# The end of norm 2 and the first gate products in another written order

## The chip, the cores and the metric

One core of a Trainium2 chip runs the kernel. The metric is the device time of one execution in microseconds (us). Before the change the median of three timed executions is 1270.69 us (1270.49 to 1272.03).

## The reference

One decoder layer on 1024 rows of 1024 numbers in float32. What matters here is its second half:

```
x = x + einsum('bse,ed->bsd', mixed, w_out)        # output projection, residual
h = rms_norm(x, ffn_norm_g)                        # norm 2
g = einsum('bsd,df->bsf', h, w_gate)
u = einsum('bsd,df->bsf', h, w_up)
x = x + einsum('bsf,fd->bsd', silu(g) * u, w_down)
return rms_norm(x, final_norm_g)
```

with 2816 hidden columns. Ahead of it stand norm 1, the input projection and two kinds of attention.

## The kernel before

*Split operands.* Every float32 operand of a product is split in two: a high part (a cast on ScalarE, name ending in h) and a low part (the operand less its high part, ending in l). A product is then three matmuls per 128 rows of the contraction: high by high, high by low, low by high. `operand` (L705) does it for a weight block (oh, ol), `hi_part` and `lo_part` (L744, L747) for a row block's slice of a large operand.

*Gate and up products.* They go by pairs of 128 hidden columns, 11 pairs, gate (m = 0) and up (m = 1). Each is a Strassen scheme of seven products instead of eight. h, transposed, is seen as 2 by 2 halves: r12 and r22 hold h12 and h22, and the seven right-hand operands are 11, 21, 22, T1 = h12 - h11, T2 = h22 - T1, T3 = h22 - h12 and T4 = h21 - T2; each has a high and a low tile. `product` (L865) runs twelve matmuls (contraction 512, 512 rows) into one PSUM bank. The left-hand operands are four weight blocks a11, a21, a12, a22 and sums s1, s2 of them, made on GpSimd. `strassen` (L951) does a pair; the first pair is done by `strassen_first` (L970), for which the products on 22 and T3 of both m run ahead ("held"), as they need only the upper four row blocks.

*Norm 2.* The loop from L830 goes over the row blocks (128 rows) in the order 7, 6, 5, 4, 0, 1, 2, 3. Step n does the second half of the output projection for its block (two banks of twelve matmuls), adds the residual on VectorE, squares and sums on ScalarE (L135), raises to the power -1/2 on GpSimd (L137), and, one step later, scales (`normed`, L822, two halves; the gain lies in two PSUM banks, g_at). Two steps later TensorE transposes the block (`transposed`, L753, four 128 by 128 transposes to a bank) and `second_half` (blocks 4 to 7) or `first_half` (0 to 3) makes the operands; part of that runs later, on GpSimd (`late`). `first_half_below` (L787) makes 21 and T4. `early_sum` (L799) makes weight sums for the held products, in between.

*PSUM.* Eight banks: three in ps_s, two in ps_p, two in ps_t and one in ps_v. g_at holds the one of ps_v and one of ps_t until the last `normed`. After norm 2 the last three become ps_d.

*What sets the order.* Inside `tc.manual_schedule` (L829 to L901) the instructions of TensorE, VectorE, ScalarE and GpSimd run on each engine in the order in which the program writes them; each engine takes its queue strictly in that order. Outside it a planner at compile time orders them by its own estimates. DMA issues on SP's queue are left to the planner throughout: a load waits for its buffer (two buffers, tag wr, for weights).

Of the kernel before, what the change touches and what calls it, by code (L numbers as in the profile page):

```python
# [11 lines left out]
F32 = mybir.dt.float32  # L12
F32R = mybir.dt.float32r
AF = mybir.ActivationFunctionType
ALU = mybir.AluOpType
# [57 lines left out]
def layer(ctx: ExitStack, tc: tile.TileContext, x, mix_g, w_in, b_forget, lq1, lk1, lq2, lk2,  # L73
# [687 lines left out]
    def second_half(t, pvs):  # L761

        A.copy(at(r12, t), pvs[0])
        hi_part("22", t, pvs[1])
        A.copy(at(r22, t), pvs[1])
        t3 = temp(t % 2 * 2)
        V.tensor_sub(t3, pvs[1], at(r12, t))
        lo_part("22", t, pvs[1], V)
        hi_part("T3", t, t3)
        return lambda: lo_part("T3", t, t3, G)  # L770

    def first_half(t, pvs):


        hi_part("11", t, pvs[0])
        t1 = temp(t % 2 * 2)
        V.tensor_sub(t1, at(r12, t), pvs[0])
        lo_part("11", t, pvs[0], V)
        hi_part("T1", t, t1)

        def pool():
            G.tensor_sub(at(r22, t), at(r22, t), t1)
# [12 lines left out]


    w_first, w_sums, early = {}, {}, [[], []]
# [19 lines left out]
    for nh in range(2):  # L817
        A.copy(g_at[nh], gb2[:, nh * 512:nh * 512 + 512])
    temps.append(bp.tile([P, 2, 512], F32, tag="b", name="temps"))
    rs = {}  # L820

    def normed(tb):  # L822
        for nh in range(2):
            cs = slice(nh * 512, nh * 512 + 512)
            V.scalar_tensor_tensor(xns[tb][:, cs], x2[tb // 2][:, tb % 2, cs], rs[tb], g_at[nh],
                                   ALU.mult, ALU.mult)

    manual = tc.manual_schedule(engines=NORM_MAN)
    manual.__enter__()  # L829
    for n, tb in enumerate(order):  # L830
        xt = x2[tb // 2][:, tb % 2]
        for nh in range(2):
            cs = slice(nh * 512, nh * 512 + 512)
            ps = ps_s.tile([P, 512], F32, tag="s", name="pso")
            out_matmuls((4, 5, 6, 7), w2[nh], tb, ps)
            if nh == 0 and n >= 2:
                t = order[n - 2]
                pvs = [transposed(t, q) for q in range(2 if t >= 4 else 1)]
            V.tensor_add(xt[:, cs], ps, xa_half(tb, nh))
            if nh == 0:  # L840
                if n >= 1:
                    normed(order[n - 1])
                if n >= 2:
                    late = (second_half if t >= 4 else first_half)(t, pvs)
                if plan.get(n - 1, (0, 0))[1]:
                    early[plan[n - 1][0]].append(operand(temp(1)))
# [4 lines left out]
        if n >= 2:  # L851
            late()
        if n in plan:
            early_sum(*plan[n])
        if n == 1:
# [27 lines left out]
    pvs = [transposed(2, 0)]  # L883
    normed(3)
    first_half(2, pvs)()
    held[0][1] = product(early[0][1], "T3", SS)
    pvs = [transposed(3, 0)]
    first_half(3, pvs)()
    a_first = [operand(w_first[0][0])]
    for t in range(4):  # L890
        lo_part("T2", t, at(r22, t), G)
    held[1][0] = product(early[1][0], "22", SS)
    pvs = [transposed(t, 1) for t in (0, 1)]
    for t in (0, 1):
        first_half_below(t, pvs[t])
    held[1][1] = product(early[1][1], "T3", PJ)
    pvs = [transposed(t, 1, (TT, PJ)) for t in (2, 3)]
    a_first.append(operand(w_first[0][2]))
    for t in (2, 3):
        first_half_below(t, pvs[t - 2])  # L900
# [68 lines left out]

    def strassen_first(takes):  # L970

        for m, take in enumerate(takes):
            a11, a21, a12, a22 = w_blocks(m, 0) if m else w_first[0]
            s1, s2 = w_sums[m]
            p1, u2, u3 = kept_tiles()
            A.copy(p1, product(a_first[0] if m == 0 else operand(a11), "11"))
            take(0, 0, product(a_first[1] if m == 0 else operand(a12), "21"), p1)
            ps5 = product(operand(s1), "T1")
            ps = product(operand(s2), "T2")
# [5 lines left out]
            take(1, 0, product(operand(a22), "T4"), u3)  # L985

    for pair in range(NF // 2):
        me = V if pair == NF // 2 - 1 else G
# [253 lines left out]
```

## Time and profile before

| | us |
|---|---|
| median of 3 timed runs | 1270.69 |
| the profiled execution | 1268.52 |
| its span, first to last instruction | 1266.8 |
| TensorE busy | 1222.2 (96%) |
| VectorE busy | 857.3 (68%) |
| GpSimd busy | 710.5 (56%) |
| ScalarE busy | 576.1 (45%) |

The changed stage lies between 554 and about 664 us of the span: the loop over row blocks to 604, the held products and what is left of the operands to 629, the first pair to 663. A matmul's busy time overlaps the next one's, so a start-to-start distance is the better measure. An entry of a timeline ends with the idle time of the engine ahead of it and the instruction that ended the wait.

### The profile page before, as it was taken

What the parts mean: (1) busy time and instruction counts of PE and PEld (TensorE: products, weight loads), DVE (VectorE), ACT (ScalarE), POOL (GpSimd) and SP (SyncE); (2) the same over time, 40 slices, a digit from 0 to 9 for tenths busy, and PEclk for the clock granted to TensorE, in tenths of its full rate; (3) what the DMA queues carried; (4) which work ended last, traced back from release to release, by engine and by line L of the source; (5) the groups of instructions that cost most, each with busy time, mean ns of one, the idle gap of its engine ahead of it and who ended that gap; (6) DMA issues with size and microseconds to landing.
All of it is one profiled execution on the core that took longest, in us unless ns stands there. A gap on an engine that the chain in (4) does not pass through costs nothing.

```text
span 1266.8 us, 18426 instructions
## 1 busy us (share of the span) xinstructions
PE 1222.2 (96%) x6341; PEld 1039.2 (82%) x6341; DVE 857.3 (68%) x1617; ACT 576.1 (45%) x1227; POOL 710.5 (56%) x653
## 2 busy tenths in 40 slices
PE   8999999999999998989699999999999998999997
PEld 7889988987898877878578888888888886788886
DVE  5556766757786789757656565566565668878765
ACT  5345546646675666545433332233332345434424
POOL 2322333233104363235558777777777758999973
PEclk9999999999999999999999999999999999999999
DMA  6231223031202234032123443323233357735313
GB/s 217 64 109 43 72 69 84 26 98 45 51 8 80 59 137 175 14 117 96 37 89 111 133 144 123 100 83 109 100 108 124 101 183 236 219 119 179 98 57 133
DMA packets 93373, 131.42 MB, mean 104 GB/s; under 512 B 7584, under 2 KB 56288, under 8 KB 93280
## 3 DMA queue, kind: packets, MB, share of 16 engines
q1 hardware_dynamic: 91984, 126.32, 31.2%
q10 hardware_dynamic: 1296, 3.94, 0.8%
q8 instruction: 50, 0.82, 0.3%
q14 instruction: 43, 0.35, 0.1%
HBM read 93.75 MB, written 30.18 MB: 98 GB/s over the span
## 4 chain that ended last, share of the span: by engine, by line
PE 81%; POOL 6%; DVE 5%; issue 3%; DMA 3%; ACT 2%; SPq 0%; POOLq 0%; ACTq 0%; DVEq 0%
PE pst L873 31%; PE psd L1095 14%; PE psv L230 6%; PE pso L602 4%; PE pv L375 4%; PE tp L390 3%; PE s L330 2%; PE s L331 2%; POOL unit L1066 2%; POOL tw L1050 1%; PE psq_f1q L293 1%; PE psq_d2q L293 1%; PE psq_f2q L293 1%; PE psq_d3k L293 1%; PE psq_f1k L293 1%
## 5 line engine op out<-in xcount | busy, mean ns | idle before, releaser
L1095 PE MATMUL psd<-unit 128*128 128x512 f32 x924 | 211.5, 390 | 4.9 <-DVE x L1107 3.9
L1095 PEld LDWEIGHTS psd<-unit 128*128 128x128 f32 x924 | 172.8, 188 | 43.4 <-DVE x L1107 5.2
L1066 DVE TENSOR_TENSOR unit<-araw,unit 128x512 fp32r<-128x512 f32 x77 | 104.3, 1383 | 32.4 <-ACT unit L1065 19.8
L710 DVE TENSOR_TENSOR ol<-st,oh 128x512 fp32r<-128x512 f32 x84 | 91.2, 1087 | 42.8 <-ACT oh L709 41.6
L334 ACT ACTIVATE pt<-pt,mn 128x896 f32<-128x896 f32 (+7 forms) x128 | 99.4, 777 | 44.1 <-DVE mn L332 42.0
L709 ACT CAST oh<-st 128x512 fp32r<-128x512 f32 x84 | 50.9, 619 | 148.9 <-POOL st L724 108.6
L397 DVE TENSOR_TENSOR pl<-tp,ph 128x512 fp32r<-128x512 f32 (+1 forms) x120 | 75.2, 633 | 44.9 <-ACT ph L396 44.2
L396 ACT CAST ph<-tp 128x512 fp32r<-128x512 f32 (+1 forms) x120 | 64.1, 541 | 62.6 <-PE tp L390 53.7
L997 POOL TENSOR_TENSOR sg<-sg,cc 128x512 f32<-128x512 f32 x44 | 65.8, 1496 | 43.6 <-ACT sg L996 37.9
L710 DVE TENSOR_TENSOR ol<-raw,oh 128x512 fp32r<-128x512 f32 x66 | 64.9, 984 | 35.1 <-ACT oh L709 35.0
L1065 ACT CAST unit<-araw 128x512 fp32r<-128x512 f32 x77 | 47.4, 619 | 75.2 <-PE psd L1095 40.6
L422 POOL TENSOR_SCALAR_AFFINE_SELECT cb<-cb 128x128 f32<-128x128 f32 x64 | 21.9, 344 | 99.2 <-DVE mn L332 63.4
L709 ACT CAST oh<-raw 128x512 fp32r<-128x512 f32 x66 | 40.8, 619 | 80.1 <-PE pst L873 76.1
L1003 POOL TENSOR_TENSOR sg<-sg,cc 128x512 f32<-128x512 f32 x40 | 59.5, 1489 | 30.1 <-DVE cc L1002 30.1
L724 POOL TENSOR_TENSOR st<-raw 128x512 f32<-128x512 f32 x42 | 54.8, 1305 | 30.7 <-DMA raw<-in_w_gate_dram 18.5
L394 POOL MEMSET ph<- 128x128 f32 x48 | 9.8, 205 | 106.5 <-PE pv L375 100.4
L390 PE MATMUL tp<-ident,pt 128*128 128x128 f32 x432 | 67.2, 274 | 2.1 <-DVE pt L475 1.8
L127 POOL TENSOR_TENSOR wl<-wr,wh 128x1024 fp32r<-128x1024 f32 x26 | 64.5, 2481 | 1.4
L390 PEld LDWEIGHTS tp<-ident,pt 128*128 128x128 f32 x432 | 51.1, 141 | 7.4 <-issue 1.8
L126 POOL TENSOR_SCALAR wh<-wr 128x1024 fp32r<-128x1024 f32 x26 | 27.8, 1069 | 52.3 <-PE psq_f2k L293 13.8
L230 PE MATMUL psv<-wh,hh 128*128 128x256 f32 x192 | 55.0, 287 | 0.1
L230 PE MATMUL psv<-wl,hh 128*128 128x256 f32 x192 | 54.7, 285 | 0.0
(386 smaller groups left out, 3842.6 us busy)
## 6 DMA issues: line engine op xcount, KB each, us to landing
araw<-act_d SPq DMA_DIRECT2D x77, 256.0 KB, 2.7
raw<-in_w_gate_dram SPq DMA_DIRECT2D x24, 512.0 KB, 3.6
raw<-in_w_up_dram SPq DMA_DIRECT2D x24, 512.0 KB, 3.7
wr<-in_w_in_dram SPq DMA_DIRECT2D x22, 512.0 KB, 4.0
act_d<-sa SPq DMA_DIRECT2D x44, 256.0 KB, 2.5
wraw<-in_w_down_dram SPq DMA_DIRECT2D x40, 256.0 KB, 4.2
act_d<-sg SPq DMA_DIRECT2D x33, 256.0 KB, 2.1
xt<-in_x_dram SPq DMA_DIRECT2D x8, 512.0 KB, 5.8
```

Of the source, the lines that this page charges most:

```text
L127: lo_eng.tensor_tensor(lo[:, :n], raw[:, :n], hi[:, :n].bitcast(F32), ALU.subtract)
L230: T.matmul(ps[:, :n], hslice(l, dt, tb), r, start=(k == 0), stop=(k == 23))
L334: A.activation(pt[:, :L], pt[:, :L], AF.Exp, bias=mn[:, nb - 1:nb], scale=-1.0, accum_out=mn[:, 2:3])
L390: T.transpose(tp[:, a * 256 + b * P:a * 256 + (b + 1) * P], pts[b][:, sb * P:(sb + 1) * P], ident)
L396: A.copy(ph[:, o:], tp[:, o:])
L397: V.tensor_sub(pl[:, o:], tp[:, o:], ph[:, o:].bitcast(F32))
L709: A.copy(h, src)
L710: V.tensor_sub(l, src, h.bitcast(F32))
L873: T.matmul(ps, l[:, j], r[:, j], start=(k == 0), stop=(k == 11))
L997: G.tensor_mul(sg, sg, g)
L1066: lo = le.tensor_tensor(u[:, 2 * k + 1], src, u[:, 2 * k].bitcast(F32), ALU.subtract)
L1095: T.matmul(open_banks[i, m], l, r, start=(k == 0 and not top), stop=(k == last), skip_group_check=top)
```

## The change

In the loop: the scale of the first block reads the gain from memory (gb2), and the two copies of the gain into PSUM are written at the end of step 1, not ahead of the loop. The add of the second half stands ahead of the early weight sum's split, and in step 7 ahead of block 1's operands too. Of the deferred part of the operands, the first piece (the low part of T3, or r22 less T1) is written ahead of the power of rstd in steps 2 to 6 and behind it in step 7. `first_half` no longer casts T2; the casts of T2 are written later.

After the loop: transposes, casts and held products are written in another order, with banks given. 21's low part is written ahead of T4. T4's low parts of blocks 0 and 1 go to GpSimd; T4 has four temporaries in place of two. a22, s1 and s2 are split ahead of the first pair. The transposes of blocks 2 and 3 (lower half) use ps_t alone.

The first pair: each product has a bank given, in the order 11, 21, T1, T2, T4; up's weight blocks are loaded and split inside the gate's steps; the written order ends after the gate's products (m = 0), not ahead of the pair.

```diff
@@ first_half / first_half_below
-        def pool():
-            G.tensor_sub(at(r22, t), at(r22, t), t1)
-            lo_part("T1", t, t1, G)
-            hi_part("T2", t, at(r22, t))
-        return pool
+        return (lambda: G.tensor_sub(at(r22, t), at(r22, t), t1),
+                lambda: lo_part("T1", t, t1, G))
-    def first_half_below(t, pv):
-        t4 = temp(t % 2 * 2 + 1)
-        hi_part("21", t, pv)
-        V.tensor_sub(t4, pv, at(r22, t))
-        lo_part("21", t, pv, V)
-        hi_part("T4", t, t4)
-        lo_part("T4", t, t4, V)
+    def first_half_below(t, pv, step=None):
+        if step is not True:
+            hi_part("21", t, pv)
+            lo_part("21", t, pv, V)
+        if step is False:
+            return
+        t4s[t] = temp((1, 3, 0, 2)[t])
+        V.tensor_sub(t4s[t], pv, at(r22, t))
+        hi_part("T4", t, t4s[t])
@@ normed
-            V.scalar_tensor_tensor(..., rs[tb], g_at[nh], ...)
+            V.scalar_tensor_tensor(..., rs[tb], gb2[:, cs] if tb == order[0] else g_at[nh], ...)
@@ loop (both projections of the step stand ahead of this)
+        V.tensor_add(xt[:, :512], pss[0], xa_half(tb, 0))
+        if n >= 1:
+            normed(order[n - 1])
+        if n == 7:
+            V.tensor_add(xt[:, 512:], pss[1], xa_half(tb, 1))
+        if n >= 2:
+            late = (second_half if t >= 4 else first_half)(t, pvs)
+        if n < 7:
+            V.tensor_add(xt[:, 512:], pss[1], xa_half(tb, 1))
+        if 2 <= n < 7:
+            late[0]()
         xns[tb] = pp.tile([P, D], F32, tag="p", name="xn")
         rs[tb] = rstd_of(xt, xns[tb], sm)
+        if n == 7:
+            late[0]()
+        if n >= 2:
+            late[1]()
+        if plan.get(n - 1, (0, 0))[1]:
+            early[plan[n - 1][0]].append(operand(temp(1)))
+        if n == 1:
+            for nh in range(2):
+                A.copy(g_at[nh], gb2[:, nh * 512:nh * 512 + 512])
...
+        if n == 6:
+            hi_part("T2", t, at(r22, t))
@@ after the loop, as it stands after the change
     held[0][0] = product(early[0][0], "22", SS)
     normed(3)
+    pv2 = transposed(2, 0, (PJ,))
     held[0][1] = product(early[0][1], "T3", SS)
+    late2 = first_half(2, [pv2])
+    pv3 = transposed(3, 0, (TT,))
+    pv0 = transposed(0, 1, (PJ,))
+    held[1][0] = product(early[1][0], "22", SS)
+    late3 = first_half(3, [pv3])
+    for step in late2 + late3:
+        step()
     a_first = [operand(w_first[0][0])]
+    for t in (1, 2, 3):
+        hi_part("T2", t, at(r22, t))
     for t in range(4):
         lo_part("T2", t, at(r22, t), G)
+    pv1 = transposed(1, 1, (TT,))
+    held[1][1] = product(early[1][1], "T3", PJ)
+    first_half_below(0, pv0)
+    pvs = [transposed(t, 1, (TT,)) for t in (2, 3)]
+    a_first.append(operand(w_first[0][2]))
+    first_half_below(1, pv1)
     for t in (0, 1):
+        lo_part("T4", t, t4s[t], G)
+    first_half_below(2, pvs[0], False)
+    first_half_below(3, pvs[1])
+    first_half_below(2, pvs[0], True)
+    a_first.append(operand(w_first[0][3]))
+    a_first.append(operand(w_sums[0][0]))
     for t in (2, 3):
+        lo_part("T4", t, t4s[t], V)
-    manual.__exit__(None, None, None)
     norms.close()
...
+    a_first.append(operand(w_sums[0][1]))
@@ strassen_first
+        ops, D = a_first, (ps_d, "d")
+        for m, (take, banks) in enumerate(zip(takes, ((PJ, D, D, D, PJ), (D, SS, D, SS, PJ)))):
...
+            A.copy(p1, product(ops[0], "11", banks[0]))
+            ps = product(ops[1], "21", banks[1])
+            ps5 = product(ops[3] if len(ops) > 3 else operand(s1), "T1", banks[2])
+            take(0, 0, ps, p1)
+            ps = product(ops[4] if len(ops) > 4 else operand(s2), "T2", banks[3])
+            if m == 0:
+                a11, a21, a12, a22 = w_blocks(1, 0)
+                nxt = [operand(a11), operand(a12)]
             V.tensor_add(u2, ps, p1)
...
+            ps = product(ops[2], "T4", banks[4])
+            if m == 0:
+                ops = nxt + [operand(a22), operand(w_sums[1][0])]
+            take(1, 0, ps, u3)
+            if m == 0:
+                manual.__exit__(None, None, None)
```

## Rows read from the trace of the kernel before

**Rows 1.** The page, parts 1 and 4: busy time by engine, and the chain.

```profile
...
PE 1222.2 (96%) x6341; PEld 1039.2 (82%) x6341; DVE 857.3 (68%) x1617; ACT 576.1 (45%) x1227; POOL 710.5 (56%) x653
...
PE 81%; POOL 6%; DVE 5%; issue 3%; DMA 3%; ACT 2%; SPq 0%; POOLq 0%; ACTq 0%; DVEq 0%
```

**Rows 2.** Windows: stretch, its length, busy by engine (instructions), granted clock, DMA share, GB/s.

```profile
...
630.00:637.00 7.00, 7.00 (x24) 5.58 (x23) 3.45 (x6) 2.37 (x5) 0.00 (x0) 0.72 0.26 79
637.00:664.00 27.00, 25.69 (x111) 20.28 (x110) 17.10 (x21) 11.31 (x19) 16.02 (x12) 1.00 0.25 77
664.00:700.00 36.00, 36.00 (x160) 29.66 (x159) 23.95 (x32) 11.26 (x19) 29.84 (x21) 1.00 0.32 110
```

**Rows 3.** Timeline of TensorE: start, duration (us), engine, line, operation, count, [idle before <- releaser].

```profile
...
570.46 0.63 PE L758 MATMUL pt<-ident,xn 128*128 128x128 f32 x4 [1.32 <-DVE xn L825]
...
604.53 0.39 PE L873 MATMUL pst<-h22h,oh 128*128 128x512 f32 x1
...
607.25 0.60 PE L758 MATMUL pt<-ident,xn 128*128 128x128 f32 x4
607.61 0.48 PE L873 MATMUL pst<-T3h,oh 128*128 128x512 f32 x1
...
612.02 0.63 PE L758 MATMUL pt<-ident,xn 128*128 128x128 f32 x4 [1.40 <-DVE xn L825]
...
618.24 0.47 PE L873 MATMUL pst<-T3h,oh 128*128 128x512 f32 x1 [1.95 <-DVE 11l L749]
...
628.96 0.80 PE L873 MATMUL pst<-21h,oh 128*128 128x512 f32 x1 [6.25 <-DVE ol L710]
...
634.36 0.40 PE L873 MATMUL pst<-11h,oh 128*128 128x512 f32 x1
...
653.88 0.51 PE L873 MATMUL pst<-T2h,oh 128*128 128x512 f32 x1 [0.48 <-ACT oh L709]
...
663.50 0.50 PE L873 MATMUL pst<-11h,oh 128*128 128x512 f32 x1 [0.78 <-DVE kept L980]
```

**Rows 4.** Timeline of VectorE, 569 to 630, the same columns.

```profile
...
569.17 0.48 DVE L502 SCALAR_TENSOR_TENSOR mix<-o,g,rp 128x256 f32<-128x256 f32 x1
569.57 0.74 DVE L825 SCALAR_TENSOR_TENSOR xn<-x,ss,g_at 128x512 f32<-128x512 f32 x1
...
607.75 0.69 DVE L710 TENSOR_TENSOR ol<-temps,oh 128x512 fp32r<-128x512 f32 x1 [0.74 <-ACT oh L709]
608.36 0.69 DVE L839 TENSOR_TENSOR x<-pso,x 128x512 f32<-128x512 f32 x1
611.12 1.41 DVE L825 SCALAR_TENSOR_TENSOR xn<-x,ss,g_at 128x512 f32<-128x512 f32 x2 [2.08 <-POOL ss L137]
...
622.03 1.64 DVE L749 TENSOR_TENSOR T4l<-temps,T4h 128x512 fp32r<-128x512 f32 x1
...
629.49 0.68 DVE L749 TENSOR_TENSOR T4l<-temps,T4h 128x512 fp32r<-128x512 f32 x1
```

**Rows 5.** Timeline of ScalarE, 568 to 610.

```profile
...
568.35 0.58 ACT L818 COPY g_at<-gb 128x512 f32<-128x512 f32 x1
...
609.08 1.06 ACT L135 ACTIVATE xn<-x 128x1024 f32<-128x1024 f32 x1 [1.36 <-DVE x L839]
```

**Rows 6.** Timeline of GpSimd, 611 to 626.

```profile
...
612.28 1.29 POOL L749 TENSOR_TENSOR T1l<-temps,T1h 128x512 fp32r<-128x512 f32 x1
...
620.06 5.96 POOL L749 TENSOR_TENSOR T2l<-r,T2h 128x512 fp32r<-128x512 f32 x4
```

**Rows 7.** The page, part 6: loads, KB each, median us to landing.

```profile
...
raw<-in_w_up_dram SPq DMA_DIRECT2D x24, 512.0 KB, 3.7
```

**Rows 8.** Windows around three gaps of TensorE, for the granted clock.

```profile
...
552.00:554.00 2.00, 2.00 (x9) 1.70 (x9) 1.21 (x5) 0.78 (x2) 0.74 (x1) 0.51 0.97 321
626.00:630.00 4.00, 1.04 (x3) 0.85 (x4) 4.00 (x7) 2.06 (x4) 0.01 (x1) 0.64 0.00 0
1066.00:1070.00 4.00, 0.97 (x4) 0.84 (x5) 4.00 (x5) 3.79 (x8) 4.00 (x4) 1.00 0.52 171
```

More of the change, by code (lines that the diff above doesn't have):

```diff
@@ L769, in second_half @@
         hi_part("T3", t, t3)
-        return lambda: lo_part("T3", t, t3, G)
+        return lambda: lo_part("T3", t, t3, G), lambda: None
     def first_half(t, pvs):
@@ L816, in layer @@
     g_at = [pool.tile([P, 512], F32, tag=tag, name="g_at") for pool, tag in ((ps_v, "pv"), (ps_t, "t"))]
-    for nh in range(2):
-        A.copy(g_at[nh], gb2[:, nh * 512:nh * 512 + 512])
     temps.append(bp.tile([P, 2, 512], F32, tag="b", name="temps"))
@@ L824, in normed @@
             cs = slice(nh * 512, nh * 512 + 512)
-            V.scalar_tensor_tensor(xns[tb][:, cs], x2[tb // 2][:, tb % 2, cs], rs[tb], g_at[nh],
-                                   ALU.mult, ALU.mult)
+            V.scalar_tensor_tensor(xns[tb][:, cs], x2[tb // 2][:, tb % 2, cs], rs[tb],
+                                   gb2[:, cs] if tb == order[0] else g_at[nh], ALU.mult, ALU.mult)
     manual = tc.manual_schedule(engines=NORM_MAN)
@@ L831, in layer @@
         xt = x2[tb // 2][:, tb % 2]
+        t, pss = order[n - 2] if n >= 2 else None, []
         for nh in range(2):
-            cs = slice(nh * 512, nh * 512 + 512)
-            ps = ps_s.tile([P, 512], F32, tag="s", name="pso")
-            out_matmuls((4, 5, 6, 7), w2[nh], tb, ps)
+            pss.append(ps_s.tile([P, 512], F32, tag="s", name="pso"))
+            out_matmuls((4, 5, 6, 7), w2[nh], tb, pss[nh])
             if nh == 0 and n >= 2:
-                t = order[n - 2]
                 pvs = [transposed(t, q) for q in range(2 if t >= 4 else 1)]
[L839 to L846, printed above, removed]
+        V.tensor_add(xt[:, :512], pss[0], xa_half(tb, 0))
[9 more added lines that the diff above has]
+            late[0]()
         xns[tb] = pp.tile([P, D], F32, tag="p", name="xn")
         rs[tb] = rstd_of(xt, xns[tb], sm)
+        if n == 7:
[7 more added lines that the diff above has]
+                A.copy(g_at[nh], gb2[:, nh * 512:nh * 512 + 512])
         if tb >= 4:
             nc.scalar.dma_start(out=x2_d[(tb - 4) * P:(tb - 3) * P, :], in_=xt)
-        if n >= 2:
-            late()
+        if n == 6:
+            hi_part("T2", t, at(r22, t))
         if n in plan:
@@ L882, in layer @@
     held[0][0] = product(early[0][0], "22", SS)
-    pvs = [transposed(2, 0)]
     normed(3)
-    first_half(2, pvs)()
+    pv2 = transposed(2, 0, (PJ,))
     held[0][1] = product(early[0][1], "T3", SS)
-    pvs = [transposed(3, 0)]
-    first_half(3, pvs)()
+    late2 = first_half(2, [pv2])
[5 more added lines that the diff above has]
+        step()
     a_first = [operand(w_first[0][0])]
+    for t in (1, 2, 3):
+        hi_part("T2", t, at(r22, t))
     for t in range(4):
         lo_part("T2", t, at(r22, t), G)
-    held[1][0] = product(early[1][0], "22", SS)
-    pvs = [transposed(t, 1) for t in (0, 1)]
-    for t in (0, 1):
[L895 to L898, printed above, removed]
+    pv1 = transposed(1, 1, (TT,))
[4 more added lines that the diff above has]
+    first_half_below(1, pv1)
+    for t in (0, 1):
+        lo_part("T4", t, t4s[t], G)
[4 more added lines that the diff above has]
+    a_first.append(operand(w_sums[0][0]))
     for t in (2, 3):
-        first_half_below(t, pvs[t - 2])
-    manual.__exit__(None, None, None)
+        lo_part("T4", t, t4s[t], V)
     norms.close()
@@ L970, in strassen_first @@
     def strassen_first(takes):
-        for m, take in enumerate(takes):
-            a11, a21, a12, a22 = w_blocks(m, 0) if m else w_first[0]
+        ops, D = a_first, (ps_d, "d")
+        for m, (take, banks) in enumerate(zip(takes, ((PJ, D, D, D, PJ), (D, SS, D, SS, PJ)))):
             s1, s2 = w_sums[m]
             p1, u2, u3 = kept_tiles()
[L976 to L979, printed above, removed]
+            A.copy(p1, product(ops[0], "11", banks[0]))
[6 more added lines that the diff above has]
+                nxt = [operand(a11), operand(a12)]
             V.tensor_add(u2, ps, p1)
@@ L984, in strassen_first @@
             take(0, 1, held[m][0], u2)
-            take(1, 0, product(operand(a22), "T4"), u3)
+            ps = product(ops[2], "T4", banks[4])
[4 more added lines that the diff above has]
+                manual.__exit__(None, None, None)
     for pair in range(NF // 2):
```

1 line of the change is left out of this document (added).

## Prediction

> **What bounds the kernel now.** I read the page first: TensorE is busy 96% of the span and 81% of the chain that ended last, the others share the rest [rows 1]. So time can only be won where TensorE stands still or runs slowly. Then the windows: from 664 us on TensorE is busy for all of every stretch at full clock, but between 630 and 664 it is neither, with a granted clock of 0.72 in the first 7 us [rows 2]. The timeline of TensorE then shows where the changed stage stops: it waits at 570.46 (1.32 us, for norm 2 of row block 7), 612.02 (1.40, for norm 2 of block 3), 618.24 (1.95, for a bank that VectorE had to read out), 628.96 (6.25, for operands of h21) and 663.50 (0.78) [rows 3].
>
> How much is that in all? Twelve matmuls of one product begin at 604.53 and the next thing at 607.25, so a product is 2.72 us or 0.227 us a matmul; four transposes take 0.36 us (607.25 to 607.61) [rows 3]. Between 604.53 and 663.50, counting the timeline, there are 15 products (180 matmuls) and six groups of four transposes: 40.8 + 2.2 = 43.0 us of work in 58.97 us. So 15.9 us are lost in this stretch: the waits, the gaps around them, and 13 matmuls from 628.96 to 634.36 that take 5.40 us for 2.95, because the clock had fallen from 2.4 to 1.2 GHz (0.42 us a matmul), which is 2.45 us [rows 3].
>
> **The change part by part.** No arithmetic is added: the same casts, subtractions, transposes and products are issued. Only their order moves, and four low parts change engine or place. I follow it from the front.
>
> *Gain scale read from memory for the first block, copies into PSUM behind block 6's Square.* The second half of block 7's norm ran at 569.57, after the copy at 568.35 that waits for a bank [rows 4, 5]; now it needs no copy and follows its first half, some 6 us earlier. TensorE's transposes of 570.46 then wait at most for their own bank, which the attention's last read leaves at 569.65 (569.17 + 0.48) [rows 4]. Gain between 0 (something of the attention's tail takes the place) and 1.65 (no wait); I take 0.8, the bank's. From there to 604.53 TensorE had no gap, and the per-block chain (Square to the next norm 2.04 us, from 609.08 to 611.12, plus the adds and reads) gets shorter, because the split of an early weight sum (on VectorE at 607.75, 0.69) no longer stands ahead of the second half's add (608.36) [rows 4, 5]. The low part of T3 now stands ahead of the power on GpSimd, but is done while ScalarE squares: nothing. So the held products start at 603.7.
>
> *The last block's chain.* VectorE adds its second half at 603.9 instead of 608.36. Then T1 of block 1 (0.69) and its cast (0.62) on ScalarE stand ahead of Square: 605.8. Plus 2.04 gives 607.8; the early sum's split (0.60) stands ahead: norm from 608.45, first half done at 609.2 (0.74 [rows 4]). TensorE wants it after two products and a transpose group, at 609.5. The wait of 612.02 is gone. The wait of 618.24 goes too: h11's and T1's reads of that bank end at 611, its product comes at 613.
>
> *h21 and T4.* TensorE has four products and five transpose groups: 603.7 + 10.9 + 1.8 = 616.4. The sixth group (block 3, lower half) needs a bank of the pool of two that block 1's lower half holds until T4 of block 1 is subtracted. That follows a chain in the new written order. Norm done 609.8; T1 of block 2 subtracted at 610.45; GpSimd then has r22 of block 2, the low part of T1 and r22 of block 3, three operations of 1.27 (1.29 with its end, at 612.28) [rows 6]: 614.3; ScalarE casts T2 of block 3 (0.62), which stands ahead of the first h21 cast (0.58): 615.45; VectorE h21's low part (0.60) and T4 of block 0 (0.69): 616.75; ScalarE T4's cast, the split of a12 and h21 of block 1 (0.62, 0.52, 0.52): 618.4; VectorE the split's low part, h21's low part, T4 of block 1: 620.8. The low part of a12 has both inputs in SBUF and meets GpSimd's T2 low parts (four, 5.96 us); the nearest row is the T4 low part of 622.03, which took 1.64 beside them, against 0.68 at 629.49 with GpSimd idle [rows 4, 6]. I take 1.6 (0.6 would bring 619.8).
>
> The Trainium skill, "SBUF — State Buffer", section "Who interferes with whom", says the same of these two engines: a VectorE instruction with two SBUF inputs and a GpSimd one that reads SBUF do not share, the later of them waits for the whole other instruction. By it T4's low parts of blocks 0 and 1, now on GpSimd, could block VectorE as well; the trace bears the rule out at 622.03, and by it the sum would lose another 1.3 us at most if one more split on the chain met one.
>
> So TensorE waits 4.4 us for that group (616.4 to 620.85) where it waited 6.25 for operands: the wait moves to an earlier place and shrinks, but doesn't go. Then product 11 runs 621.2 to 623.9. Product 21 needs its bank: VectorE takes low parts of h21 of blocks 2 and 3 and T4 of 3 and 2, four of 0.60, done at 624.4: 0.5 lost. Splits of a22, s1, T4's low parts and s2 follow at 626.1, 626.7, 627.9 and 628.5, and their products start at 632.6, 627.15 and 629.9 (s2): all in time. Nothing else is queued behind these waits but the first sigmoid.
>
> *Order kept through the gate products; loads of the up weights.* The two loads on SP's queue wait for the two weight buffers, free when a11 (about 612) and a22 (626.1) are split; with 3.7 us to land [rows 7] the second is there at 629.8, and its splits are wanted from 631 on. ScalarE's queue has them behind the first sigmoid, ahead of the others: cover about 2 us. The up products follow at 635; the next pair's second load can start at 637 and lands 10 us ahead of its use. Cost nothing; if the cover is gone, up to 3 us.
>
> *Sum.* Gain 0.8, plus 15.9 lost in the old stretch, less 4.4 + 0.5 + 0.3 (what two restarts of TensorE add) = 5.2 in the new: 11.5 us. Open is the clock after the wait of 4.4. After 6.25 us it fell, as the 626 to 630 window shows (0.64); in the 4 us from 1066, with TensorE busy 0.97, it stayed at 1.00; at 552, behind a stretch of sparse work, it stood at 0.51 [rows 8]. The price lies between 0 and the 2.45 of before; a wait of 4.4 lies between 6.25 and those 3, so I take half: 1.2. That leaves 10.3 us, 0.8%. From 664 on TensorE is the bound through the pairs [rows 2] and what it feeds moves with it, so the gain reaches the end. The profiled execution took 1268.52 (span 1266.8 and 1.7 around it); 1258.2 of that kind. The median of the timed runs is 2.2 above it, 1270.69: I predict 1260.4.
>
> **Rivals.**
> *The waits come back in the first pair* (up weights late, the next pair's sums late on GpSimd, or splits slowed by its products). For it: the old stage waited 0.48 at 653.88 and 0.78 at 663.50 on just such splits and reads [rows 3], and GpSimd was busy 16 of the 27 us to 664 [rows 2]. Against: the cover above. Price 3 to 7 us of the 10.3: 1263 to 1268.
>
> *It does nothing*: what TensorE saves here it waits for in the next pairs or in the switch to the down projection. For it: in that switch TensorE stands and GpSimd is busy without a break (4.00 of 4 us from 1066 [rows 8]). Against: TensorE is busy in all of 664 to 700, so nothing there waits for a fixed time, and those loads wait for buffers that TensorE frees. 1268 to 1273.
>
> *Slower*: one mechanism, the clock. The new order puts short waits ahead of products 11, 21, T1, T2 and T4 (a bank or an operand just in time); if TensorE, at half clock from the 4.4 us wait, doesn't come back before they end, each matmul costs 0.2 us more. From 58 matmuls on (11.5 / 0.2, five of the ten products) the gain is gone; all 120 cost 24 us, thus about 1283. For it: 0.51 at 552 after a sparse stretch. Against: before, full clock was back at 634.36 with unbroken products [rows 3], and the waits that I find between these are 0.5 us or less.
>
> *More*: the pool hands block 3's group another bank, or a12's split meets no GpSimd work: the wait shrinks to 2 us or less, gain 14 and more, 1256 or less.
>
> **How the numbers follow.** Forecast 0.66 (own range 1256.5 to 1264), waits in the first pair 0.13, more 0.05, nothing 0.07, slower 0.09. A change under 0.2% (2.5 us) can't be told from none here. Faster: 0.66 + 0.13 + 0.05 = 0.84; same 0.07; slower 0.09. Low end 1255 (a gain of 15.7, nearly all of what is lost), high end 1267 (the first rival's most).
>
> **What would show it.** Product 22 on held operands starts near 603.7; the norm of block 3 runs at 608 to 610 instead of 611.1; there is no wait ahead of block 3's upper transposes nor ahead of the second T3 product; one wait of 3 to 5 us stands ahead of block 3's lower transposes, ended by a VectorE subtraction T4; product 11 starts near 621, and the eleventh product from there ends near 652 in place of 663.5. Wrong it would be if TensorE's wait there is over 6 us or under 2, if the granted clock is down for more than a product after it, or if the stretches after 660 have waits that they had not.

## The result and the profile after

| | before | after |
|---|---|---|
| median of 7 timed runs, us | 1272.97 (1270.49 to 1275.81) | 1264.89 (1259.56 to 1268.87) |
| ratio, 95% interval | | 0.9937 [0.9919, 0.9955] |
| the profiled execution | 1268.52 | 1264.89 |

The change gains 8.1 us in this series, between 5.7 and 10.3 by the interval. A later series of six runs of the same kernel on another chip gave 0.9954 [0.9936, 0.9971], or 5.9 us. The forecast time was 1260.4, a gain of 10.3; the measured median lies outside the forecast's own range (1256.5 to 1264) and inside the whole one (1255 to 1267).

The page of the kernel after, parts 1 and 4, answers to [rows 1]: TensorE has 85% of the chain in place of 81%.

```profile
...
PE 1225.3 (97%) x6341; PEld 1043.4 (83%) x6341; DVE 867.9 (69%) x1615; ACT 573.4 (45%) x1227; POOL 714.1 (57%) x655
...
PE 85%; DVE 4%; POOL 4%; DMA 3%; ACT 2%; issue 2%; SPq 0%; POOLq 0%; ACTq 0%; DVEq 0%
```

TensorE's timeline of the kernel after (columns as in [rows 3]), first at the end of the attention, then around the changed stage:

```profile
...
568.78 0.60 PE L758 MATMUL pt<-ident,xn 128*128 128x128 f32 x4
570.67 0.30 PE L500 MATMUL rp<-ident,dg 128*128 128x128 f32 x1 [1.29 <-DVE dg L494]
571.78 0.33 PE L500 MATMUL rp<-ident,dg 128*128 128x128 f32 x1 [0.81 <-DVE dg L494]
572.69 0.65 PE L758 MATMUL pt<-ident,xn 128*128 128x128 f32 x4 [0.58 <-DVE mix L502]
...
608.39 0.39 PE L883 MATMUL pst<-h22h,oh 128*128 128x512 f32 x1
...
621.16 0.60 PE L758 MATMUL pt<-ident,xn 128*128 128x128 f32 x4
625.30 1.08 PE L758 MATMUL pt<-ident,xn 128*128 128x128 f32 x4 [3.53 <-DVE temps L792]
626.03 0.78 PE L883 MATMUL pst<-11h,oh 128*128 128x512 f32 x1
...
629.90 0.39 PE L883 MATMUL pst<-21h,oh 128*128 128x512 f32 x1
```

Here one sees both halves of the result. From 608.39 on there is one wait, 3.53 us at 625.30, where before had 1.40, 1.95, 6.25 and 0.78 [rows 3]. But ahead of 572.69 there are three (1.29, 0.81, 0.58), where before had one of 1.32, and the held products begin at 608.39 in place of 604.53. The windows (columns as in [rows 2]) show a granted clock below 1.00 behind both places:

```profile
...
570.00:575.00 5.00, 2.94 (x12) 2.23 (x13) 3.97 (x8) 1.87 (x4) 1.56 (x2) 0.86 0.18 73
575.00:580.00 5.00, 5.00 (x19) 4.04 (x18) 1.54 (x3) 1.98 (x4) 1.38 (x2) 0.80 0.00 0
625.00:630.00 5.00, 4.70 (x17) 3.97 (x18) 2.73 (x5) 3.33 (x6) 3.80 (x4) 0.68 0.00 0
...
635.00:664.00 29.00, 29.00 (x129) 23.85 (x128) 19.35 (x26) 9.52 (x18) 15.42 (x12) 1.00 0.28 91
664.00:700.00 36.00, 36.00 (x160) 29.57 (x159) 26.96 (x29) 11.55 (x20) 30.75 (x22) 1.00 0.28 95
```

Before had 0.72 in 630 to 637 [rows 2]; in its front, 570 to 580, it had 1.00. The VectorE and then the GpSimd timeline of the same kernel, for the causes:

```profile
...
563.79 1.40 DVE L824 SCALAR_TENSOR_TENSOR xn<-x,ss,gb 128x512 f32<-128x512 f32 x2
...
568.98 0.69 DVE L837 TENSOR_TENSOR x<-pso,x 128x512 f32<-128x512 f32 x1 [0.22 <-PE pso L602]
569.58 0.74 DVE L824 SCALAR_TENSOR_TENSOR xn<-x,ss,g_at 128x512 f32<-128x512 f32 x1
570.24 1.49 DVE L494 TENSOR_SCALAR dg<-ones,rr 128x128 f32<-128x128 f32 x2
...
572.15 0.48 DVE L502 SCALAR_TENSOR_TENSOR mix<-o,g,rp 128x256 f32<-128x256 f32 x1
...
618.08 1.70 DVE L710 TENSOR_TENSOR ol<-raw,oh 128x512 fp32r<-128x512 f32 x1 [0.60 <-ACT oh L709]
...
622.89 1.06 DVE L710 TENSOR_TENSOR ol<-raw,oh 128x512 fp32r<-128x512 f32 x1 [1.21 <-ACT oh L709]
...
624.48 0.68 DVE L792 TENSOR_TENSOR temps<-pt,r 128x512 f32<-128x512 f32 x1
```

```profile
...
567.80 0.55 POOL L137 TENSOR_TENSOR ss<-ss,mhalf 128x1 f32<-128x1 f32 x1 [5.04 <-ACT ss L136]
...
568.98 1.27 POOL L724 TENSOR_TENSOR st<-raw 128x512 f32<-128x512 f32 x1
570.33 1.32 POOL L724 TENSOR_TENSOR st<-st,raw 128x512 f32<-128x512 f32 x1
```

The kernel before, on the same two engines:

```profile
...
568.27 0.48 DVE L494 TENSOR_SCALAR dg<-ones,rr 128x128 f32<-128x128 f32 x2 [0.27 <-POOL rr L492]
```

```profile
...
572.41 0.55 POOL L137 TENSOR_TENSOR ss<-ss,mhalf 128x1 f32<-128x1 f32 x1 [4.18 <-ACT ss L136]
...
572.92 1.30 POOL L724 TENSOR_TENSOR st<-raw 128x512 f32<-128x512 f32 x1
```

Absolute times can't be compared between profiles: the attention's end moves by up to 5.4 us from one execution to the next (its last sp matmuls of L489 ahead of 560 begin at 551.3 to 556.7 in the profiles here). So I compare durations of stages, read off TensorE's timelines. "Front" goes from the first transposes of row block 7 to the first held product; "stage" from there over 180 product matmuls (58.97 us in the prediction's count); "pairs" on to the first matmul of the down projection; "down" to its last. The last column is the first product behind the stage's longest wait (21 in before, f1, e3, e5, e6, e7 and f4, else 11): 2.72 us at full clock, 5.1 to 5.3 at half.

| profile | front | stage | pairs | down | longest wait | product behind it |
|---|---|---|---|---|---|---|
| before | 36.51 | 58.97 | 379.83 | 216.40 | 6.25 | 5.2 |
| before again (f1) | 36.50 | 59.02 | 379.83 | 218.73 | 6.24 | 5.1 |
| after | 39.61 | 48.91 | 379.74 | 219.04 | 3.53 | 3.87 |
| after again (f2) | 39.61 | 49.01 | 380.40 | 218.01 | 3.51 | 4.00 |
| e1 gain copied ahead | 36.51 | 48.99 | 380.22 | 219.98 | 3.5 | 3.98 |
| e2 first sums later | 38.59 | 48.91 | 380.40 | 219.50 | 3.5 | 3.90 |
| e3 before + gain edit | 39.58 | 59.32 | 379.79 | 217.71 | 5.30 | 5.2 |
| e4 h21, T4 as before | 39.62 | 50.68 | 380.28 | - | 3.96 | 5.19 |
| e5 order ends early | 39.61 | 50.70 | 379.69 | 218.27 | 3.14 | 5.25 |
| e6 lower halves first | 39.62 | 46.01 | 380.23 | 219.29 | 1.49 | 2.85 |
| e7 e6 + copies ahead | 36.51 | 46.00 | 379.75 | 218.75 | 1.44 | 2.84 |
| e8 block 3 as the others | 39.63 | 48.08 | 380.22 | 219.63 | 2.48 | 4.43 |
| f3 one cast moved | 39.58 | 50.22 | 380.58 | 217.47 | 3.51 | 5.19 |
| f4 e7 + that cast | 36.50 | 46.03 | 379.77 | 217.60 | 1.47 | 2.84 |

e4's profiled execution was a slow one: its down projection, 233 us long, is not compared (the dash), and the run stands in none of e4's times below.

Between executions of one kernel the front repeats within 0.1 us, the pairs within 0.7, the down projection within 2.3, and the stage within 0.1, but for f3, which has after's order up to there and took 1.3 more. The change brings +10.06 in the stage (10.01 by the repeats) and -3.10 in front: 7.0 us, inside both intervals.

### The profile page after: what moved, and what is told of

The parts are those of the page before. It is cut to its first block, busy times and chain, and to the rows that moved or that the text cites. A ratio compares the mean times of both kernels' runs of the same rounds, so it can differ in the third digit from the quotient of the medians.

```text
span 1263.2 us, 18426 instructions
## 1 busy us (share of the span) xinstructions
PE 1225.3 (97%) x6341; PEld 1043.4 (83%) x6341; DVE 867.9 (69%) x1615; ACT 573.4 (45%) x1227; POOL 714.1 (57%) x655
## 4 chain that ended last, share of the span: by engine, by line
PE 85%; DVE 4%; POOL 4%; DMA 3%; ACT 2%; issue 2%; SPq 0%; POOLq 0%; ACTq 0%; DVEq 0%
PE pst L883 31%; PE psd L1125 14%; PE pso L602 7%; PE psv L230 6%; PE pv L375 4%; PE tp L390 3%; PE s L330 2%; PE s L331 2%; POOL unit L1096 1%; PE psq_f1q L293 1%; PE psq_d2q L293 1%; DMA araw<-act_d 1%; PE psq_f2q L293 1%; PE psq_d3k L293 1%; PE psq_f1k L293 1%
## 5 line engine op out<-in xcount | busy, mean ns | idle before, releaser
L710 DVE TENSOR_TENSOR ol<-st,oh 128x512 fp32r<-128x512 f32 x84 | 95.4, 1138 | 73.1 <-ACT oh L709 71.7
L710 DVE TENSOR_TENSOR ol<-raw,oh 128x512 fp32r<-128x512 f32 x66 | 74.8, 1139 | 20.6 <-ACT oh L709 20.3
```

The lines of the kernel that those rows point to most:

```text
L710: V.tensor_sub(l, src, h.bitcast(F32))
```

## The experiments

All were timed against the kernel before; ratios are to it, with 95% intervals. The first four shared one chip, e5 to e8 another, f1 to f4 a third.

### e1, e2, e3: the front

e1 undoes the gain edit in the kernel after, e3 makes it alone in the kernel before. e2 leaves the edit and moves the first early weight sum from step 1 to step 2.

```diff
 e1 (from the kernel after)
+    for nh in range(2):                       # ahead of the loop
+        A.copy(g_at[nh], gb2[:, nh * 512:nh * 512 + 512])
-        if n == 1: (the two copies)
-            ... gb2[:, cs] if tb == order[0] else g_at[nh] ...
+            ... g_at[nh] ...
 e2 (from the kernel after)
-        if n in plan:
-            early_sum(*plan[n])
+        if n == 2:
+            early_sum(*plan[1])
+        if n in plan and n != 1:
+            early_sum(*plan[n])
 e3 (from the kernel before): the reverse of e1's edit
```

> The changed kernel with one edit undone: the copies of the gain into PSUM stand ahead of the loop again, and the first block's norm reads them. In the changed kernel's trace the held products started at 608.4 us, 3.9 later than before, where 603.7 was forecast. Theory: block 6's earlier Square let GpSimd begin the first two weight sums at 569.0 instead of 572.9, in the middle of the attention's last block; VectorE's two dg instructions took 1.49 us beside them instead of 0.48, TensorE waited 1.29 + 0.81 + 0.58 us for them and their reader, and its clock then fell. By it the held products start at 604 to 605 here, the granted clock of 570 to 580 is 1.00, and the time is 3 us under the changed kernel's (0.991 of the kernel before). Rival: the late start is chance (a cold clock at 554 us in that one execution); then the start is anywhere, and the ratio stays 0.9937.

> The changed kernel with the first two weight sums written one step of the loop later (behind step 2's power on GpSimd); the gain edit stays. Theory as in the run with the copies ahead: with GpSimd free, dg takes 0.48 us again, the held products start at 603.7 to 604.5, and the time is 3 to 4 us under the changed kernel's (ratio 0.990 to 0.991). Rival 1: TensorE's wait at 570 comes from the gain edit itself (the bank, or VectorE's norm ahead of dg), not from GpSimd; then the wait stays and the ratio is 0.9937. Rival 2: the sums, later, hold up the power of the next steps; then TensorE gets gaps between 575 and 605.

> The kernel before with the gain edit alone (first block's norm reads the gain from memory, copies behind block 6's Square). The forecast costed it at a gain of 0.8 us (0 to 1.65). Theory: here too Square of block 6 runs early, the two weight sums start near 569 and meet dg; TensorE's wait near 570 is longer and its clock may fall: 1 to 4 us slower than before (1.001 to 1.003). By the forecast: 0.8 us faster.

| | median, us | ratio |
|---|---|---|
| e1 | 1264.11 (1262.88 to 1266.04) | 0.9934 [0.9920, 0.9947] |
| e2 | 1265.31 (1263.40 to 1268.15) | 0.9943 [0.9927, 0.9958] |
| e3 | 1275.68 (1273.90 to 1278.66) | 1.0026 [1.0017, 1.0035] |

The gain edit alone makes the kernel slower: 3.07 us in front by e3's profile, 2.2 to 4.5 by its interval. Undone, the front is back at 36.51 with a granted clock of 1.00. e1's median does not stand clear of after's: the 3 us that were expected of it show in its front and not in its time, whose runs spread over 3 us. In e7 below the same undoing brings 3.5 us in the medians against e6 of the same series. e1 and e3 also part the change in two: without the gain edit the stage still takes 48.99, and with that edit alone 59.32. So the 10 us come from the other edits.

Where do the 3.1 us come from? The attention's tail is a short chain: VectorE writes "dg" (row factors), TensorE transposes it (rp, L500), and VectorE's mix (L502) reads rp. Block 7's norm, which waits no longer for a copy, runs as a whole at 563.79. All that follows it in the loop comes earlier with it: in VectorE's rows above, the next step's add (568.98) and the first half of block 6's norm (569.58) now stand ahead of the attention's last dg (570.24), for which TensorE waits. Before, that dg came first, at 568.27. And the pair of dg takes 1.49 us in place of 0.48: GpSimd's second early sum (570.33) has begun, and the second dg ends at 571.73, just after that sum at 571.65. Before, block 6's power stood at 572.41 and the first sum at 572.92; now the power comes at 567.80 and the sum right behind the attention's own work, 4.7 us earlier when counted from block 7's first transposes. The Trainium skill, "SBUF — State Buffer", section "Who interferes with whom", says that a tensor_scalar on VectorE in a two-port mode shares a port pair with GpSimd, and that whoever has it second waits for the other's whole instruction. The end times agree; that dg runs in such a mode no run shows. In e2 GpSimd is idle there, with VectorE's order unchanged:

```profile
...
572.14 0.69 DVE L837 TENSOR_TENSOR x<-pso,x 128x512 f32<-128x512 f32 x1 [0.22 <-PE pso L602]
572.75 0.74 DVE L824 SCALAR_TENSOR_TENSOR xn<-x,ss,g_at 128x512 f32<-128x512 f32 x1
573.40 0.48 DVE L494 TENSOR_SCALAR dg<-ones,rr 128x128 f32<-128x128 f32 x2
```

The dg take 0.48 again, and the distance between block 7's first and second transposes falls from 3.91 to 2.90 (before: 2.44). So 1.0 us of the loss is the collision, 0.5 the order. The other 1.6 is the clock: in e2, too, 35.69 us pass from the second transposes to the held products, against 34.07 before and in e1. The windows of e2 and then of e1 show it:

```profile
...
575.00:580.00 5.00, 5.00 (x18) 4.00 (x18) 2.19 (x5) 2.32 (x5) 1.28 (x1) 0.66 0.00 0
```

```profile
...
570.00:580.00 10.00, 8.60 (x47) 6.98 (x46) 7.32 (x15) 5.15 (x11) 4.58 (x5) 1.00 0.13 52
```

The clock fell behind two gaps (1.29 and 0.57 in e2) or three in a stretch of short matmuls; behind the single gap of 1.32 in before and e1 it stayed at 1.00. So e2's expectation, 3 to 4 us back, was wrong: 1.0 came back, and the rest goes with its rival 1 (VectorE's norm ahead of dg), by the order and the clock.

### e4 and e5: two parts of the stage

e4 puts h21 and T4 back (per block: 21h, T4, 21l, T4h, T4l, all low parts on VectorE, in the old places). e5 ends the written order ahead of the first pair.

```diff
 e4 (from the kernel after), first_half_below and its calls as before:
-    def first_half_below(t, pv, step=None): ...
+    def first_half_below(t, pv):
+        t4 = temp(t % 2 * 2 + 1)
+        hi_part("21", t, pv); V.tensor_sub(t4, pv, at(r22, t))
+        lo_part("21", t, pv, V); hi_part("T4", t, t4); lo_part("T4", t, t4, V)
 e5
         lo_part("T4", t, t4s[t], V)
+    manual.__exit__(None, None, None)
     norms.close()
 ...
-            if m == 0:
-                manual.__exit__(None, None, None)
```

> The changed kernel with the old order of the lower half: T4 subtracted ahead of 21's low part, all T4 low parts on VectorE block by block, two temporaries. By the forecast's chain two T4 low parts of 1.6 us beside GpSimd's T2 low parts, less 0.6 for the low part of 21, stand ahead of T4 of block 1 or behind it: the wait ahead of block 3's lower transposes grows from 3.5 to about 5.5 us, and products 21 and T4 wait besides: 3 to 6 us above the changed kernel (ratio 0.996 to 0.998). Rival: the wait is set by GpSimd's subtractions of r22 and ScalarE's cast of T2 of block 3 alone; then it stays at 3.5 and the time within 1 us.

> The changed kernel, but the written order ends ahead of the first pair again, so that the planner orders the pair's products. Measured by the stretch from the first held product to the first matmul of the down projection: 438.8 us before, 428.7 in the changed kernel (429.2 and 429.3 in two variants with the same code there). Theory: the 10 us come from the operands' order (no wait at 612 and 618, one of 3.5 for 6.25), and the written order of the pair gives at most the 1.3 us that the old one waited inside the pair (0.48 and 0.78): 429 to 431 here. Rival: the written order of the pair is the main part, since the planner lets product 21 begin ahead of 11 and TensorE then stands at its operands: 434 or more.

e4: 1267.95 us (1264.45 to 1271.03), 0.9961 [0.9948, 0.9975]; e5: 1267.23 us (1265.74 to 1270.29), 0.9960 [0.9947, 0.9973]. TensorE's timeline of e4 and then of e5:

```profile
...
628.11 1.09 PE L758 MATMUL pt<-ident,xn 128*128 128x128 f32 x4 [3.96 <-DVE 21l L749]
628.85 0.78 PE L881 MATMUL pst<-11h,oh 128*128 128x512 f32 x1
...
634.04 0.39 PE L881 MATMUL pst<-21h,oh 128*128 128x512 f32 x1
```

```profile
...
625.20 0.63 PE L758 MATMUL pt<-ident,xn 128*128 128x128 f32 x4 [0.53 <-DVE temps L792]
628.97 0.77 PE L883 MATMUL pst<-21h,oh 128*128 128x512 f32 x1 [3.14 <-DVE temps L792]
```

Both lose 1.8 us of the stage. In e4 the wait for the same transposes is 0.4 longer, ended by a low part of 21, and the product behind it takes 5.19 in place of 3.87. In e5 the planner puts product 11 ahead of the transposes, and 21 then waits 3.14 with half the clock behind it. By these numbers 1.3 to 1.4 of the 1.8 us are the price of the clock, which, as f3 shows below, differs by 1.3 us between executions of one and the same order; with one profile each, 0.4 to 0.5 us remain as the order's own. e4's expectation (a wait of 5.5, 3 to 6 us) was wrong: the old order of T4 costs the wait next to nothing. e5's was right (430.4 us from the held products to the down projection, 429 to 431 expected). The rest of the 10 us comes from the transposes and the held products standing in another order, which no run took apart further.

### e6, e7, e8: the wait that was left

e6 writes 21 and T4 of blocks 0 and 1 ahead of the weight splits and the casts of T2; e7 is e6 with e1's edit. e8 gives the last block's step the order of the others (operands and deferred part ahead of its second add).

```diff
 e6
+    pv1 = transposed(1, 1, (TT,))
+    for t, pv in ((0, pv0), (1, pv1)):
+        hi_part("21", t, pv)
+    for t, pv in ((0, pv0), (1, pv1)):
+        lo_part("21", t, pv, V)
+        t4s[t] = temp((1, 3)[t]); V.tensor_sub(t4s[t], pv, at(r22, t))
     a_first = [operand(w_first[0][0])]
-    (T2 casts and low parts, pv1)
     held[1][1] = product(early[1][1], "T3", PJ)
-    first_half_below(0, pv0)
     pvs = [transposed(t, 1, (TT,)) for t in (2, 3)]
+    for t in (0, 1):
+        hi_part("T4", t, t4s[t])
     a_first.append(operand(w_first[0][2]))
-    first_half_below(1, pv1)
+    (T2 casts, T2 low parts, T4 low parts of 0 and 1 on GpSimd)
 e8
-        if n == 7:
-            V.tensor_add(xt[:, 512:], pss[1], xa_half(tb, 1))
 ...
-        if n < 7:
-            V.tensor_add(xt[:, 512:], pss[1], xa_half(tb, 1))
-        if 2 <= n < 7:
+        V.tensor_add(xt[:, 512:], pss[1], xa_half(tb, 1))
+        if 2 <= n:
             late[0]()
```

> The changed kernel with another order behind the upper halves: ScalarE casts h21 of blocks 0 and 1, and VectorE makes their low parts and T4, ahead of the splits of a11 and a12 and of the casts of T2. Theory (the chain of the forecast): the 3.53 us wait ahead of block 3's lower transposes was set by T2's cast of block 3, which waits for three GpSimd operations, and by the splits, standing ahead of h21 on ScalarE and VectorE. Here T4 of block 1 is done about 5 us earlier, at the time TensorE gets there: a wait of 0.5 us or less, no fall of the granted clock near 625, the stretch from the held products to the down projection 424 to 425 us instead of 428.7, the time 4 to 5 us under the changed kernel's (ratio 0.990). Rival: the wait moves to the products of 11, 21 or T2, whose splits and low parts come later now: 427 to 429.

> The last order, and the gain edit undone. Both parts add: 3.1 us from the start of the held products (block 7's second transposes to the first held product 34.1 us instead of 35.7, the two transposes 2.4 apart instead of 3.9) and 4 to 5 us behind it: 7 to 8 us under the changed kernel's, ratio 0.987 to 0.988, if the switch to the down projection doesn't take part of it back (it took 2.6 us there). If the gain edit costs nothing in the mean of many executions, it is level with the last one.

> The changed kernel with the last block treated as the others: its second half is added behind block 1's operands, and r22 of block 1 is subtracted ahead of the power. Its add then comes 1.2 us later (two VectorE instructions of 0.60), but Square no longer waits for T1's cast (0.62), and the power may wait for GpSimd's subtraction: norm 2 of block 3 is 0.5 to 1.5 us later. TensorE wanted it with 0.3 us to spare: by the theory a wait of 0 to 1.2 us ahead of block 3's upper transposes and the wait ahead of its lower ones shorter or longer by as much, the time 0 to 1.5 us above the changed kernel's. Rival: this edit carries much of the 10 us; then the stretch from the held products on is over 432.

| | median, us | ratio |
|---|---|---|
| e6 | 1264.01 (1261.44 to 1266.40) | 0.9928 [0.9911, 0.9945] |
| e7 | 1260.52 (1256.97 to 1263.05) | 0.9898 [0.9879, 0.9917] |
| e8 | 1266.52 (1264.37 to 1267.45) | 0.9948 [0.9932, 0.9963] |

TensorE's timeline and one window of e6:

```profile
...
624.85 1.03 PE L758 MATMUL pt<-ident,xn 128*128 128x128 f32 x8
625.64 0.48 PE L883 MATMUL pst<-11h,oh 128*128 128x512 f32 x1
...
630.11 0.47 PE L883 MATMUL pst<-21h,oh 128*128 128x512 f32 x1 [1.49 <-DVE temps L792]
...
632.96 0.39 PE L883 MATMUL pst<-T1h,oh 128*128 128x512 f32 x1
```

```profile
...
630.00:635.00 5.00, 4.71 (x19) 3.60 (x20) 3.83 (x5) 3.95 (x7) 3.14 (x3) 1.00 0.34 95
```

The eight transposes run without a wait. Part of it comes back ahead of product 21 (1.49, for T4 of blocks 2 and 3), but the clock stays at 1.00 and the product behind takes 2.85. The stage is 2.9 us shorter; up to the down projection it is 426.2 us where 424 to 425 was expected. This shows the forecast's cause of the wait: the bank that block 1's lower half holds until its T4 is subtracted. With the front's 3.1 us as well, e7 beats both kernels, by 13 us over before; its ratio is a little short of the 0.987 to 0.988 that was expected. TensorE's timeline of e8:

```profile
...
624.44 0.63 PE L758 MATMUL pt<-ident,xn 128*128 128x128 f32 x4 [2.48 <-DVE temps L792]
624.83 0.68 PE L878 MATMUL pst<-11h,oh 128*128 128x512 f32 x1
```

Without "the last block's chain first" the wait is 2.48, not longer: the stage is 0.8 us shorter than after's, though the clock behind costs more. The special order of the last step is thus worth nothing here: block 3's norm begins 3.9 us after the first held product without it and 4.6 with it (6.6 before), and its transposes wait in neither. What both have and before has not is the second add ahead of the early sum's split, which is probably what brought it forward; no run moved that add alone.

### f1 to f4: the switch to the down projection

In the first profiles the down projection took 2.6 us more after the change, with a wait of 1.91 that before had not. f1 and f2 are the two kernels once more. f3 and f4 move one low part, for which VectorE stood 3.9 us behind a load ahead of the last pair's reads, to GpSimd, in after and in e7.

```diff
 f3, f4
-            for k, (src, le) in enumerate(((raw, V), (self.right(pair, bn), G))):
+            for k, (src, le) in enumerate(((raw, G if Chunk.units == 4 else V), (self.right(pair, bn), G))):
```

> The kernel before once more, to see how far its stages repeat from execution to execution. In the first profile of before, the stretch from the first matmul of the down projection to the last of them takes 216.4 us, with one wait of 3.14 near 1069 and none ahead of it; in the six profiles of kernels with the changed stage it takes 218.3 to 220.0, with a wait of 1.6 to 2.5 some 13 us after its start. Theory A (the change pushes a wait into the switch to the down projection): 216 to 217 here again. Theory B (that stretch differs from execution to execution, whatever the kernel): 218 or more here, with a wait at its start.

> The changed kernel once more. From its first held product to the down projection 428.7 us as in the first profile (within 0.5); from there to the end 219 to 220 by theory A (the wait comes with the kernel), 216 to 217 by theory B (it comes with the execution). In front: 3.91 from the first transposes of row block 7 to the second, and 35.7 from there to the held products.

> The changed kernel, with one instruction moved: the low part of the fourth operand unit of the down projection, for which VectorE stood from 1029.0 to 1032.92 behind a load while the last pair's products were waiting to be read (T1's product was done near 1029), is made on GpSimd. The order of all else is the same. Theory A1 (VectorE's stand is the cause: the last pair's reads and sums come late, their store too, and SyncE's queue has the reload of the next unit behind that store): VectorE reads T1's product near 1029.7, the last store goes out 2 to 4 us earlier, the wait of 1.91 near 1050 and the half clock behind it go, and the stretch from the first matmul of the down projection to the end falls from 219.0 to 216 to 217.5; the median 1.5 to 3 us below the changed kernel. Rival A2 (the transfers are the limit: they are busy 0.83 to 0.95 there, so the unit comes when it comes): the wait stays over 1.2 and the median within 0.7 us.

> The same move on top of the fastest kernel so far (lower halves first, gain copied ahead of the loop; 1260.5): by A1 the wait of 1.62 near 1046 goes and the median falls by 1.5 to 2.5 us, to about 1258.5, 14 to 15 us below the kernel before; by A2 it stays within 0.7 us of 1260.5.

TensorE in the switch: before, before again, after.

```profile
...
1043.33 22.57 PE L1095 MATMUL psd<-unit 128*128 128x512 f32 x98
1069.03 3.01 PE L1095 MATMUL psd<-unit 128*128 128x512 f32 x12 [3.14 <-DVE x L1107]
```

```profile
...
1044.27 11.04 PE L1095 MATMUL psd<-unit 128*128 128x512 f32 x48
1056.96 12.11 PE L1095 MATMUL psd<-unit 128*128 128x512 f32 x50 [1.65 <-ACT unit L1065]
1072.21 7.98 PE L1095 MATMUL psd<-unit 128*128 128x512 f32 x28 [3.13 <-DVE x L1107]
```

```profile
...
1037.04 11.04 PE L1125 MATMUL psd<-unit 128*128 128x512 f32 x48
1049.99 13.27 PE L1125 MATMUL psd<-unit 128*128 128x512 f32 x50 [1.91 <-ACT unit L1095]
1065.38 3.01 PE L1125 MATMUL psd<-unit 128*128 128x512 f32 x12 [2.12 <-DVE x L1137]
```

f1's one timed execution took 1271.80 us. The kernel before has only the later wait of 3.14 there in one execution and one of 1.65 ahead of it in the next; the stretch takes 216.40 and 218.73, and after's again 218.01. Theory B holds: what looked like a give-back lies within what executions differ by. Over all profiles without f3's move that first wait runs from none (before), 0.41 (e3), 0.88 (f2) and 1.15 (e5) to 2.73 (e1); the stretch takes 216.4 to 218.7 in the three with the old stage and 218.0 to 220.0 in the eight with the new one that can be compared. f2: 1267.50 us (1264.77 to 1269.15).

f3 gave 1265.89 us, 0.9948 [0.9930, 0.9966], f4 1260.01, 0.9894 [0.9876, 0.9913]. In f3 the first wait is 0.35 + 0.27 in place of 1.91 (f2, without the move: 0.88 + 0.39), and the stretch takes 217.47; in f4 217.60 after e7's 218.75. That is the direction of A1 and about its amount, but in the medians it is 0.5 (f4 to e7) and 1.6 (f3 to f2), within their spreads; A1 is not shown. f3 also shows the clock's chance. TensorE's timeline:

```profile
...
625.33 1.09 PE L758 MATMUL pt<-ident,xn 128*128 128x128 f32 x4 [3.51 <-DVE temps L792]
626.07 0.78 PE L883 MATMUL pst<-11h,oh 128*128 128x512 f32 x1
...
631.26 0.40 PE L883 MATMUL pst<-21h,oh 128*128 128x512 f32 x1
```

After the same wait as in f2 (3.51) the product takes 5.19 us, not 4.00, with an identical order up to there.

## Why the prediction was right, and where it was not

- **The stage** was right: forecast 49.4 us (43.0 of work, 5.2 lost, 1.2 for the clock), measured 48.91 and 49.01. Waits of 1.40, 1.95 and 6.25 became one, at the place foreseen, ended by the foreseen subtraction of T4 of block 1 (624.48). From the first held product that subtraction was to end 17.1 us later and ended 16.8 later. Two errors nearly cancel in the sum: wait and bank wait came 1.4 us shorter than forecast, and what is left beside work, wait and clock (restarts, products behind a transpose group) was 1.2 where 0.3 was taken.
- **The wait** was to be 4.4 and is 3.53. TensorE came there 13.1 us after the first held product, not 12.7 (a product behind a transpose group takes 2.86, not 2.72), and could leave after 16.9, not 17.15.
- **The split of a12** took 1.06 (622.89) where 1.6 was taken; the split before it, at 618.08, took 1.70 beside GpSimd.
- **The bank wait of product 21** (0.5) did not appear: half the clock made product 11 end at 629.90, after the reads of 627.65 and 628.93. The clock's price covered it.
- **The clock** in the stage cost 1.15 us of the 0 to 2.45 allowed; the other profiles with the changed stage show 1.2 to 2.5 behind waits of 2.5 to 4.0 us, and 0.1 behind 1.5 (the product behind the wait, less 2.72). My half was a fair middle, but it is a draw, not a value.
- **The gain edit** is the step that failed: +0.8 (0 to 1.65) was forecast, -3.10 measured, nearly the same in every profile with the edit but e2's (-2.08). I let TensorE's transposes wait at most for their own bank, "which the attention's last read leaves at 569.65", as if that read stayed where it was. The wait was for that bank (572.69, ended by mix), but the read had moved: it ended 3.85 us after block 7's first transposes (572.63), 1.63 before. The prediction had written beside its lower end that "something of the attention's tail takes the place", and still took zero for the floor. It did not ask what else comes earlier with block 7's norm: the next add and block 6's half norm, ahead of the dg which TensorE needs (0.5 us), and block 6's power, which starts the weight sums beside that dg (1.0). The clock behind the gaps (1.6) was in no term of the front. The Trainium skill's rule on the shared port ("SBUF — State Buffer", section "Who interferes with whom") stood in the prediction, weighed at the low parts, and not here.
- **The held products' start** at 603.7 was to come 0.8 earlier; it came 3.1 later by duration.
- **Rivals.** No waits come back in the first pair (635 to 700 is full at 1.00 in after). The sign of being wrong, waits after 660 that were not there, came in small: in seven of eleven profiles with the changed stage TensorE waits 0.2 to 0.5 us at 692 to 698, and the pairs take 0.4 to 0.8 us more; in the three with the old stage neither is there. One line of f2:

```profile
...
698.02 0.50 PE L883 MATMUL pst<-11h,oh 128*128 128x512 f32 x1 [0.37 <-DVE kept L986]
```

  Whether one of the 2 us by which down projections differ belongs to the change stays open. The slower case had the right mechanism, short waits and a fallen clock, and placed it wrong: it came in the front, at 1.6 us.

So 10.1 - 3.1 = 7.0 us in place of 10.3. The time is 4.5 us over the forecast: 2.2 is gain that did not come (8.1 by the medians, which is 1.1 more than the profiles show) and 2.3 is base, as before's median was 1270.69 in the first three runs and 1272.97 over seven. That it still lies in the whole range is owed to the size of the stage's part; the price 1263 to 1268 of the first rival was met without that rival's cause.

## What to carry to other kernels

When a wait is taken away from an instruction, look at what follows it and now comes earlier too: ahead of what it then stands in its own queue, and what it starts on another engine at the same time (here GpSimd beside VectorE). Hold a bank for as short a time as possible: reading it out ahead of work that has slack (e6) was worth 2.9 us here. And profile the kernel before twice before explaining a difference of 2 us far from the change.

## What was not expected of the hardware

- Two tensor_scalar of 128 by 128 on VectorE took 1.49 us beside a GpSimd sum and 0.48 with GpSimd idle.
- The clock's price behind the same 3.5 us wait was 1.15, 1.18, 1.26, 1.28 and 2.47 us in five executions with the same order in the stage. Behind a wait of 3.1 in the down projection the clock stayed at 1.00 in before, e5, e7 and f3 and fell in e3, f1, f2 and f4 (0.83 over the 10 us behind it in f4); in front it fell after gaps of 1.29 and 0.57 among short matmuls (e2).
- The part ahead of the changed stage, in which the order was the same, ended anywhere from 551.3 to 556.7 us. In the eight late profiles (e1 to e4, e6, e7, f2, f4; block 7's first transposes at 571.2 to 573.5) the granted clock was 0.97 or 0.98 between 400 and 500 us, in the six early ones (568.0 to 569.0) 1.00; why it falls there is open.
